# Weight sums for pairs of column tiles: made by GpSimd from loaded tiles, or made in DRAM by adding transfers and loaded as blocks

## The chip, the core and the metric

The kernel runs on one NeuronCore of a Trainium2 chip. The metric is the device time of one execution in microseconds, taken as the median of several runs. Beside it stands one profiled execution, from which all views below come.

## The reference

One layer of a hybrid decoder, 512 tokens of 1024 channels, all in float32. What matters here is which weights meet which activations:

```python
u = rmsnorm(h, norm1_g)
a_glu, q, k, v, r, g_low, gate_a, gate_b = split_cols(u @ w_in)
c = silu(layernorm(causal_dwconv(a_glu[..., :CH] * sigmoid(a_glu[..., CH:]), ...)))
y_conv = c @ w_conv_out
o = gated_linear_attention(q, k, v, log_sigmoid(g_low @ w_gate_up + b_gate) / 16)
y_gla = (headnorm(o) * silu(r)) @ w_gla_out
merged = sigmoid(gate_a) * y_conv + sigmoid(gate_b) * y_gla
h = h + merged @ w_o
u2 = rmsnorm(h, norm2_g)
z = causal_dwconv(u2 @ w_ffn_up, ...)                # 2 x 2816 columns
h = h + (silu(z[..., :F]) * z[..., F:]) @ w_ffn_down
return rmsnorm(h, final_g)
```

## The kernel before, in words

**Products.** Each float32 product is made of three matmuls: both operands are split into a high part (`hi`, a cast by ScalarE) and a low part (`lo`, a subtraction by VectorE), and `mm3` (L453 to L455) multiplies low by high, high by low and high by high into one bank. A weight comes in blocks of 128 partitions x 1024 values (512 KB): a column tile holds the 8 k-blocks of 128 output columns.

**The stream of weight blocks.** `order` lists all 202 blocks in the order of their use, by name: value, GLU, decay, the four attention heads (`w_qk`, `w_r`), the merge gates and the two branch projections (`w_gb`, `w_ga`, `w_gla`, `w_conv`), `w_o`, and three groups of `w_up` and `w_down`. `load` issues the next block's DMA on SyncE's queue into one of four `raw` buffers; `split_weight` makes its two parts into one of four `whi` and four `wlo` buffers; `weight` hands a block to TensorE's loops, splits two blocks ahead (`LOOK`), and lets `refill` load up to four blocks beyond the split ones. So a load waits for the buffer of the block four loads before it, that is, for that block's cast and subtraction.

**The pairs.** Twelve gate tiles and sixteen up-projection tiles, 14 pairs in all (six in `MERGE`, eight `w_up` pairs), are multiplied two at a time with the tokens in two halves by a scheme of seven block products in place of eight (`two_tiles`, L1174). For the tiles p and q, cut into left and right halves of their columns in the block, it needs four steps: x1 (tile p itself), x3 (two sums), x2 (a sum, and the right half of q) and x4 (one sum). In the kernel before, `load` takes both tiles of the pair into two `raw` buffers at step x1, and `two_sums` (L329) lets GpSimd make the four sums, each 128 x 512, into a third buffer and into q's left half, after the blocks are split; `two_operand` names the buffer of each step. While pairs are in the stream (`tight`), only two blocks are loaded ahead in place of four.

**Other users of the queues.** GpSimd also issues adding transfers (`accum_op=ALU.add`): the low parts of some blocks (`ADDED`, L393: the transfer adds the weight onto the negated high part), and the sums of blocks of `w_o` and `w_down` (L305, L322). It takes the inverse roots of the norms (L505, L608, L1592). SyncE issues all plain loads and the stores of the output.

**The start.** Under a hand-written order (`manual_schedule`), the first tile of x is loaded in two halves, then the first weight block in two halves (`load(2)`), the second tile of x, and two more blocks. TensorE first transposes x (L581) and multiplies as parts arrive (L667).

Of the kernel before, what the change touches and what calls it, by code (L numbers as in the profile page):

```python
# [10 lines left out]
F32 = mybir.dt.float32  # L11
# [4 lines left out]
ALU = mybir.AluOpType  # L16

P = 128
D = 1024
T = 512  # L20
# [18 lines left out]
BEHIND = [_HALVES[:3], _HALVES[3:6], _HALVES[6:9], _HALVES[9:]]  # L39
BEHIND += [[("w_conv", m, half) for m in pair for half in range(2)] for pair in O_PAIRS[:2]]  # L40
MERGE_REST = [("w_conv", m) for pair in O_PAIRS[2:] for m in pair]
LOOK = 2

ADDED = {("w_glu", 2 * k) for k in range(2, KT)} | {("w_r", m) for m in range(KT)}
# [31 lines left out]
def trunk_layer(ctx: ExitStack, tc: tile.TileContext, a: dict, out: bass.AP):  # L76
    nc = tc.nc

    def pool(name, bufs, space=None):
        kw = {"space": space} if space is not None else {}  # L80
        return ctx.enter_context(tc.tile_pool(name=name, bufs=bufs, **kw))
# [9 lines left out]
    up = pool("acts", 1)  # L91
    tp = pool("temps", 1)
    ps = pool("psum", 1, bass.MemoryType.PSUM)
    edge = ctx.enter_context(tc.tile_pool(name="edge", bufs=1, side="right"))
    heap_scope, hp = scoped("heap", 26)
    conv_scope, vp = scoped("conv", 10)
# [4 lines left out]
    def nm(s):  # L101
        return f"{s}_{next(names)}"
# [115 lines left out]
    tight = set()  # L218
    first = len(order)
# [4 lines left out]
    tight |= set(range(first, len(order)))  # L224
    order += MERGE_REST
    order += [("w_o", (O_PAIRS, step, d)) for step, d in STEPS]
    for gi, pairs in enumerate(GROUPS):
        if gi == 0:
            order += [("w_up", j) for i in pairs[0] for j in (i, FT + i)]
            first = len(order) + 6  # L230
        else:
            first = len(order)
        order += up_order(up_plan(gi))
        tight |= set(range(first, len(order)))
        order += [("w_down", (pairs, step, d)) for step, d in STEPS]
    ready, raws = [], []
    pair_raws = {}
    kept = {}
    used = [0]
    pace = [None]  # L240

    def by_halves(dst, src, parts):
        for j in range(parts):
            c = slice(j * D // parts, (j + 1) * D // parts)
            nc.sync.dma_start(dst[:, c], src[:, c])

    def load(parts=1):
        if len(raws) < len(order):
            name, j = order[len(raws)]
            if name in SEVEN:  # L250
                raws.append(load_block(name, *j))
                return
            if name == "two":
                name, p, q, part = j
                if part == "x1":
                    pair_raws[name, p] = [raw_tile() for _ in range(2)]
                    for raw, m in zip(pair_raws[name, p], (p, q)):
                        nc.sync.dma_start(raw, a[name][m])
                raws.append(None)
                return  # L260
            raw = raw_tile()
            by_halves(raw, a[name][j], parts)
            raws.append(raw)

    def refill():

        while len(raws) < len(order):
            if len(raws) >= len(ready) + (2 if len(raws) in tight else 4):
                return
            load()  # L270

    def raw_tile():
        return wp.tile([P, D], F32, tag="raw", name=nm("raw"), bufs=4)
# [36 lines left out]
    def operand(raw, pairs, step, d):  # L310

        if step == "s4":
            return kept[pairs, d, "b22"]
        if step == "n2":
            nc.vector.tensor_tensor(kept[pairs, d], kept[pairs, d], raw, ALU.add)  # L315
        return raw if step in ("a12", "n3") else kept[pairs, d]

    def sum_on(name, pairs, step, d):

        if step in ("a11", "n2"):  # L320
            nxt = block(name, pairs, d, *((0, 1) if step == "a11" else (1, 0)))
            nc.gpsimd.dma_start(kept[pairs, d], nxt, accum_op=ALU.add)  # L322

    def two_operand(name, p, q, part):

        raws = pair_raws[name, p]
        return {"x1": lambda: raws[0], "x3": lambda: raws[2], "x2": lambda: raws[1], "x4": lambda: raws[2][:, :T]}[part]()

    def two_sums(name, p, q, part):  # L329

        def add(out, x, y):
            work = nc.gpsimd.tensor_tensor(out, x, y, ALU.add)  # L332
            if name == "w_up":
                tc.keep_in_program_order(work)

        left, right = slice(0, T), slice(T, D)
        if part == "x1":
            one, two = pair_raws[name, p]
            three = raw_tile()
            pair_raws[name, p].append(three)  # L340
            add(three[:, left], one[:, left], two[:, left])
            add(three[:, right], three[:, left], two[:, right])
            add(two[:, left], two[:, left], two[:, right])
        if part == "x3":
            one, _, three = pair_raws[name, p]
            add(three[:, left], three[:, right], one[:, right])

    def split_weight(halves=False, between=None):

        if len(ready) < len(order):  # L350
            while len(raws) <= len(ready):
                load()
            raw = raws[len(ready)]
            name, spec = order[len(ready)]
            if name in SEVEN or name == "two":
                raw = operand(raw, *spec) if name in SEVEN else two_operand(*spec)
# [3 lines left out]
                nc.scalar.copy(hi, raw)  # L360
                two_low[:] = [nc.vector.tensor_tensor(lo, raw, hi.bitcast(F32), ALU.subtract)]  # L361
                with ExitStack() as order_of:
                    for ins in behind:
                        order_of.enter_context(tc.issue_after(ins.ins))
                    sum_on(name, *spec) if name in SEVEN else two_sums(*spec)
# [12 lines left out]
            lo = wp.tile([P, D], F32R, tag="wlo", name=nm("wlo"), bufs=4)  # L378
            if halves:
                ready.append((hi, lo))  # L380

                def high(c):
                    nc.scalar.copy(hi[:, c], raw[:, c])

                def low(c):
                    nc.vector.tensor_tensor(lo[:, c], raw[:, c], hi[:, c].bitcast(F32), ALU.subtract)

                cols = [slice(j * T, (j + 1) * T) for j in range(2)]
                return [[lambda c=c, part=part: part(c) for c in cols] for part in (high, low)]
            nc.scalar.copy(hi, raw)  # L390
            if (name, spec) in ADDED:
                pace[0] = nc.scalar.mul(lo, raw, -1.0)  # L392
                nc.gpsimd.dma_start(lo, a[name][spec], accum_op=ALU.add)  # L393
            else:
                pace[0] = nc.vector.tensor_tensor(lo, raw, hi.bitcast(F32), ALU.subtract)  # L395
# [153 lines left out]

    def load_x(t, parts=1):  # L550
        xs[t] = tp.tile([P, D], F32, tag="x", name=nm("x"), bufs=3)
        by_halves(xs[t], a["x"][t * P : (t + 1) * P, :], parts)

    def by_four(t):
        return t.rearrange("p (k t) -> p k t", k=4)
# [1223 lines left out]
```

## Time and profile before

| what | value |
|---|---|
| median of 3 runs | 826.51 us (826.05 to 828.54) |
| the profiled execution | 825.89 us |
| its span, first to last instruction | 824.2 us |
| granted TensorE clock | 0.999 |
| DMA packets | 30905, 106.27 MB |

The views give times in us from the start of the span. PE is TensorE, PEld its weight loads, DVE VectorE, ACT ScalarE, POOL GpSimd, SP SyncE; a q behind an engine's name is its sequencer, which waits and issues DMAs. A row of a view names line, engine, operation, the tile written and those read; an arrow in brackets names what ended the wait before it.

### The profile page before, as it was taken

Reading aid. Unit: us, or ns where it says so; the run is one execution under the profiler, and the core shown is the slowest. Engines: PE = TensorE matmul, PEld = TensorE weight load, DVE = VectorE, ACT = ScalarE, POOL = GpSimd, SP = SyncE. Lnnn points to the kernel's source line nnn. Section 1 sums busy time; section 2 is a strip of 40 time slices with the busy share of each in tenths; the row PEclk is TensorE's granted clock in tenths of the full one; section 3 lists DMA queues with packets and bytes.
Section 4 is the critical chain, followed back from the end, with each engine's and each line's share of the span. In section 5 each row is a group of like instructions: output and inputs, shape, how many; then the busy total and the mean of one; then the engine's idle time right before and its main releaser. Section 6 shows DMA issues by size and latency. Waiting matters only on the chain.

```text
span 824.2 us, 11554 instructions
## 1 busy us (share of the span) xinstructions
PE 815.3 (99%) x4321; PEld 705.2 (86%) x4321; DVE 715.7 (87%) x1161; ACT 450.2 (55%) x666; POOL 150.1 (18%) x133
## 2 busy tenths in 40 slices
PE   8999999999999999999999999999999999999996
PEld 7888888888888889999988898898889988899885
DVE  6689999999989599786788889979975999789896
ACT  6744447655654456684454546556435663456654
POOL 2000010001010213533001100230133301522012
PEclk9999999999999999999999999999999999999999
DMA  8345572563443103323647623156642457334662
GB/s 315 104 118 147 148 187 101 129 153 103 93 112 103 51 27 111 119 78 106 206 116 216 196 80 103 31 169 157 139 133 90 141 140 164 106 103 165 168 129 103
DMA packets 30905, 106.27 MB, mean 129 GB/s; under 512 B 3497, under 2 KB 3633, under 8 KB 30849
## 3 DMA queue, kind: packets, MB, share of 16 engines
q1 hardware_dynamic: 25072, 85.34, 30.4%
q0 software_dynamic: 5760, 20.19, 14.5%
q8 instruction: 34, 0.56, 0.3%
q14 instruction: 23, 0.18, 0.1%
q10 hardware_dynamic: 16, 0.00, 0.0%
HBM read 103.42 MB, written 2.10 MB: 128 GB/s over the span
## 4 chain that ended last, share of the span: by engine, by line
PE 98%; DMA 1%; ACT 0%; SPq 0%; DVE 0%; POOL 0%; issue 0%; POOLq 0%; ACTq 0%
PE mm L453 28%; PE mm L454 28%; PE mm L455 28%; PE mm L667 3%; PE ax L455 2%; PE ax L453 2%; PE ax L454 2%; PE ax L1070 1%; DMA x<-in_x_dram 1%; PE ax L1072 1%; PE ax L1051 1%; PE ax L1038 0%; PE ax L1037 0%; PE ax L534 0%; PE ax L581 0%; PE ax L1085 0%
## 5 line engine op out<-in xcount | busy, mean ns | idle before, releaser
L453 PE MATMUL mm<-uh,wlo 128*128 128x512 f32 (+1 forms) x672 | 244.5, 364 | 0.0
L454 PE MATMUL mm<-ul,whi 128*128 128x512 f32 (+1 forms) x672 | 242.3, 361 | 0.0
L455 PE MATMUL mm<-uh,whi 128*128 128x512 f32 (+1 forms) x672 | 242.1, 360 | 0.0
L455 PEld LDWEIGHTS mm<-uh,whi 128*128 128x128 f32 x672 | 126.8, 189 | 19.5
L453 PEld LDWEIGHTS mm<-uh,wlo 128*128 128x128 f32 x672 | 127.0, 189 | 18.8
L454 PEld LDWEIGHTS mm<-ul,whi 128*128 128x128 f32 x672 | 127.0, 189 | 18.6
L390 ACT CAST whi<-raw 128x1024 fp32r<-128x1024 f32 x86 | 89.9, 1048 | 59.2 <-PE mm L455 33.2
L361 DVE TENSOR_TENSOR wlo<-raw,whi 128x1024 fp32r<-128x1024 f32 x80 | 94.0, 1181 | 25.2 <-ACT whi L360 21.3
L332 POOL TENSOR_TENSOR raw<-raw,raw 128x512 f32<-128x512 f32 x42 | 67.9, 1616 | 213.9 <-DVE wlo L361 118.2
L395 DVE TENSOR_TENSOR wlo<-raw,whi 128x1024 fp32r<-128x1024 f32 x70 | 90.0, 1288 | 15.3 <-ACT whi L390 15.3
L360 ACT CAST whi<-raw 128x1024 fp32r<-128x1024 f32 x80 | 76.4, 958 | 35.7 <-PE mm L455 26.8
L791 DVE SCALAR_TENSOR_TENSOR c<-h,pp,c 128x255 f32<-128x255 f32 (+14 forms) x120 | 57.4, 478 | 3.7 <-ACT c L787 3.4
L791 DVE SCALAR_TENSOR_TENSOR c<-aside,btmp,c 128x255 f32<-128x255 f32 (+14 forms) x120 | 57.4, 478 | 2.8 <-ACT c L787 2.7
L791 DVE SCALAR_TENSOR_TENSOR aside<-h,pp,aside 128x255 f32<-128x255 f32 (+6 forms) x112 | 53.6, 478 | 0.0
L360 ACT CAST whi<-kept 128x1024 fp32r<-128x1024 f32 (+1 forms) x32 | 31.8, 997 | 31.3 <-DVE kept L315 17.3
L1503 DVE SCALAR_TENSOR_TENSOR tmp<-mm,pp,tmp 128x511 f32<-128x511 f32 (+1 forms) x56 | 41.4, 743 | 4.0 <-ACT tmp L1500 3.9
L361 DVE TENSOR_TENSOR wlo<-kept,whi 128x1024 fp32r<-128x1024 f32 (+1 forms) x32 | 36.9, 1154 | 5.1 <-ACT whi L360 5.1
L1181 ACT COPY tmp<-mm 128x256 f32<-128x256 f32 x48 | 17.7, 368 | 35.1 <-PE mm L455 34.6
L1419 DVE TENSOR_TENSOR hres<-hres,mm 128x512 f32<-128x512 f32 (+1 forms) x49 | 32.3, 671 | 3.8 <-PE mm L455 2.2
L1500 ACT ACTIVATE tmp<-mm,pp 128x512 f32<-128x512 f32 x28 | 21.8, 778 | 19.0 <-PE mm L455 18.8
L392 ACT ACTIVATE wlo<-raw 128x1024 fp32r<-128x1024 f32 x16 | 16.9, 1060 | 22.1 <-PE mm L453 22.1
L1503 DVE SCALAR_TENSOR_TENSOR tmp<-tmp,pp,tmp 128x511 f32<-128x511 f32 (+1 forms) x32 | 27.8, 888 | 0.4
(350 smaller groups left out, 1787.5 us busy)
## 6 DMA issues: line engine op xcount, KB each, us to landing
raw<-in_w_up_dram SPq DMA_DIRECT2D x44, 512.0 KB, 3.7
raw<-in_w_glu_dram SPq DMA_DIRECT2D x16, 512.0 KB, 4.8
raw<-in_w_down_dram SPq DMA_DIRECT2D x15, 512.0 KB, 4.8
kept<-in_w_down_dram POOLq DMA_DIRECT2D x10, 512.0 KB, 5.8
raw<-in_w_qk_dram SPq DMA_DIRECT2D x8, 512.0 KB, 3.4
raw<-in_w_r_dram SPq DMA_DIRECT2D x8, 512.0 KB, 4.4
wlo<-in_w_r_dram POOLq DMA_DIRECT2D x8, 512.0 KB, 7.8
raw<-in_w_gb_dram SPq DMA_DIRECT2D x8, 512.0 KB, 3.3
```

Of the source, the lines that this page charges most:

```text
L332: work = nc.gpsimd.tensor_tensor(out, x, y, ALU.add)
L360: nc.scalar.copy(hi, raw)
L361: two_low[:] = [nc.vector.tensor_tensor(lo, raw, hi.bitcast(F32), ALU.subtract)]
L390: nc.scalar.copy(hi, raw)
L395: pace[0] = nc.vector.tensor_tensor(lo, raw, hi.bitcast(F32), ALU.subtract)
L453: nc.tensor.matmul(acc, ll, rh, start=first, stop=False, **kw)
L454: nc.tensor.matmul(acc, lh, rl, start=False, stop=False, **kw)
L455: nc.tensor.matmul(acc, lh, rh, start=False, stop=last, **kw)
L667: nc.tensor.matmul(acc, act, ready[k // 2][wi][:, j], start=first, stop=last)
L791: nc.vector.scalar_tensor_tensor(out[:, j:], x[:, : half_t - j], w, out[:, j:], ALU.mult, ALU.add)
L1419: done = nc.vector.tensor_tensor(hres[t, n][:, c], hres[t, n][:, c], acc[:, c], op)
L1503: nc.vector.scalar_tensor_tensor(z[:, s:], acc[:, : T - s], w[j], z[:, s:], ALU.mult, ALU.add)
```

## The change

For each pair, a tile `s` of four blocks of 128 x 512 is set up in DRAM. `sum_two` gives four stages: two copies from DRAM to DRAM of the tiles p and q, issued on SyncE's queue; one adding transfer of 512 KB (the halves of q onto blocks 0 and 2); and two of 256 KB that add blocks of `s` onto one another, issued by GpSimd, each after the one before it has landed. `SUMS_AT` gives the block at whose use the stages begin, for each pair; the next three stages follow three blocks apart. `load_two` then loads each step's block into a `raw` buffer of its own: x1 from p, x3 from `s` in one transfer, x2 half from `s` and half from q in two transfers, x4 (256 KB) from `s`. GpSimd's sums on SBUF, `tight` and the bound of two blocks go: up to four blocks are loaded ahead everywhere. The first weight block is loaded in one transfer; the first tile of x still in two.

```diff
+SUMS_AT = (26, 30, 34, 38, 42, 46, 52, 60, 68, 76, 101, 109, 137, 145)
...
+    dp = pool("dram", 1, bass.MemoryType.DRAM)
...
-                if part == "x1":
-                    pair_raws[name, p] = [raw_tile() for _ in range(2)]
-                    for raw, m in zip(pair_raws[name, p], (p, q)):
-                        nc.sync.dma_start(raw, a[name][m])
-                raws.append(None)
+                raws.append(load_two(*j))
                 return
             raw = raw_tile()
-            by_halves(raw, a[name][j], parts)
+            nc.sync.dma_start(raw, a[name][j])
             raws.append(raw)
     def refill():
-        while len(raws) < len(order):
-            if len(raws) >= len(ready) + (2 if len(raws) in tight else 4):
-                return
+        while len(raws) < min(len(ready) + 4, len(order)):
             load()
...
-    def two_sums(name, p, q, part):
-        def add(out, x, y):
-            work = nc.gpsimd.tensor_tensor(out, x, y, ALU.add)
-            if name == "w_up":
-                tc.keep_in_program_order(work)
-        left, right = slice(0, T), slice(T, D)
-        if part == "x1":
-            one, two = pair_raws[name, p]
-            three = raw_tile()
-            pair_raws[name, p].append(three)
-            add(three[:, left], one[:, left], two[:, left])
-            add(three[:, right], three[:, left], two[:, right])
-            add(two[:, left], two[:, left], two[:, right])
-        if part == "x3":
-            one, _, three = pair_raws[name, p]
-            add(three[:, left], three[:, right], one[:, right])
+    def sum_two(name, p, q):
+        s = dp.tile([P, 4, T], F32, name=nm("sums"))
+        two_in_dram[name, p] = s
+        def copies():
+            for j, m in ((0, p), (2, q)):
+                tc.keep_in_program_order(nc.sync.dma_start(s[:, j : j + 2, :], by_two(a[name][m])))
+        def add(dst, src):
+            tc.keep_in_program_order(nc.gpsimd.dma_start(dst, src, accum_op=ALU.add))
+        return [
+            copies,
+            lambda: add(s[:, 0:4:2, :], by_two(a[name][q])),
+            lambda: add(s[:, 3, :], s[:, 0, :]),
+            lambda: add(s[:, 1, :], s[:, 3, :]),
+        ]
+    def by_two(x):
+        return x.rearrange("p (j c) -> p j c", j=2)
+    def load_two(name, p, q, part):
+        raw = raw_tile()
+        if part == "x1":
+            nc.sync.dma_start(raw, a[name][p])
+            return raw
+        s = two_in_dram[name, p]
+        if part == "x3":
+            nc.sync.dma_start(by_two(raw), s[:, 0:4:3, :])
+        if part == "x2":
+            nc.sync.dma_start(raw[:, :T], s[:, 2, :])
+            nc.sync.dma_start(raw[:, T:], a[name][q][:, T:])
+        if part == "x4":
+            raw = raw[:, :T]
+            nc.sync.dma_start(raw, s[:, 1, :])
+        return raw
+    for first, (name, p, q) in zip(SUMS_AT, twos):
+        for stage in range(4):
+            two_stages.setdefault(first + 3 * stage, []).append((name, p, q, stage))
+    def sums_in_dram():
+        for name, p, q, stage in two_stages.pop(used[0], ()):
+            if stage == 0:
+                two_jobs[name, p] = sum_two(name, p, q)
+            two_jobs[name, p][stage]()
...
         used[0] += 1
+        sums_in_dram()
         prefetch(ahead)
...
     load_x(0, 2)
-    load(2)
+    load()
     load_x(1)
```

The order in which TensorE and VectorE run their instructions is the same in both kernels; ScalarE's differs by one swap. SyncE's and GpSimd's orders differ as described.

More of the change, by code (lines that the diff above doesn't have):

```diff
@@ L217, in trunk_layer @@
     order += [("w_gb", m) for m in range(AHEAD)] + [("w_gla", m) for m in range(AHEAD - 1)]
-    tight = set()
-    first = len(order)
     for (name, p, q), behind in zip(MERGE, BEHIND):
@@ L223, in trunk_layer @@
             order += [tile[:2] for tile in behind[n : n + 1] if tile[2] == 0]
-    tight |= set(range(first, len(order)))
     order += MERGE_REST
@@ L229, in trunk_layer @@
             order += [("w_up", j) for i in pairs[0] for j in (i, FT + i)]
-            first = len(order) + 6
-        else:
-            first = len(order)
         order += up_order(up_plan(gi))
-        tight |= set(range(first, len(order)))
         order += [("w_down", (pairs, step, d)) for step, d in STEPS]
     ready, raws = [], []
-    pair_raws = {}
     kept = {}
@@ L240, in trunk_layer, with load @@
     pace = [None]
[L242 to L247, printed above, removed]
+    def load():
         if len(raws) < len(order):
@@ L322, in sum_on @@
             nc.gpsimd.dma_start(kept[pairs, d], nxt, accum_op=ALU.add)
-    def two_operand(name, p, q, part):
-        raws = pair_raws[name, p]
-        return {"x1": lambda: raws[0], "x3": lambda: raws[2], "x2": lambda: raws[1], "x4": lambda: raws[2][:, :T]}[part]()
-    def two_sums(name, p, q, part):
-        def add(out, x, y):
-            work = nc.gpsimd.tensor_tensor(out, x, y, ALU.add)
-            if name == "w_up":
-                tc.keep_in_program_order(work)
-        left, right = slice(0, T), slice(T, D)
-        if part == "x1":
-            one, two = pair_raws[name, p]
-            three = raw_tile()
-            pair_raws[name, p].append(three)
-            add(three[:, left], one[:, left], two[:, left])
-            add(three[:, right], three[:, left], two[:, right])
-            add(two[:, left], two[:, left], two[:, right])
-        if part == "x3":
-            one, _, three = pair_raws[name, p]
-            add(three[:, left], three[:, right], one[:, right])
+    two_in_dram = {}
@@ new lines, in trunk_layer @@
+    two_stages = {}
+    twos = [j[:3] for what, j in order if what == "two" and j[-1] == "x1"]
+    assert len(twos) == len(SUMS_AT)
+    for first, (name, p, q) in zip(SUMS_AT, twos):
+        for stage in range(4):
+            two_stages.setdefault(first + 3 * stage, []).append((name, p, q, stage))
+    two_jobs = {}
+    def sums_in_dram():
[3 more added lines that the diff above has]
+            two_jobs[name, p][stage]()
@@ L355, in split_weight @@
             if name in SEVEN or name == "two":
-                raw = operand(raw, *spec) if name in SEVEN else two_operand(*spec)
+                raw = operand(raw, *spec) if name in SEVEN else raw
                 n = raw.shape[-1]
@@ L361, in split_weight @@
                 two_low[:] = [nc.vector.tensor_tensor(lo, raw, hi.bitcast(F32), ALU.subtract)]
[L362 to L365, printed above, removed]
+                if name in SEVEN:
+                    sum_on(name, *spec)
                 ready.append((hi, lo))
@@ L551, in load_x @@
         xs[t] = tp.tile([P, D], F32, tag="x", name=nm("x"), bufs=3)
-        by_halves(xs[t], a["x"][t * P : (t + 1) * P, :], parts)
+        for j in range(parts):
+            c = slice(j * D // parts, (j + 1) * D // parts)
+            nc.sync.dma_start(xs[t][:, c], a["x"][t * P : (t + 1) * P, c])
     def by_four(t):
```

1 line of the change is left out of this document (removed).

## The prediction

> **What bounds the kernel now.** I read the page first: busy time per engine, then the chain that ended last.
>
> ```profile
> span 824.2 us, 11554 instructions
> ## 1 busy us (share of the span) xinstructions
> PE 815.3 (99%) x4321; PEld 705.2 (86%) x4321; DVE 715.7 (87%) x1161; ACT 450.2 (55%) x666; POOL 150.1 (18%) x133
> ...
> PE 98%; DMA 1%; ACT 0%; SPq 0%; DVE 0%; POOL 0%; issue 0%; POOLq 0%; ACTq 0%
> ```
>
> TensorE works 815.3 of 824.2 us, and 98% of the chain is its own. A busy TensorE can still wait between matmuls, so I asked the view of waits for that engine alone, over the whole span, and the same for its weight loads after the first 28 us:
>
> ```profile
> PE mm L573 <- DVE ones L546: 1.1, 1, 1.1
> PE mm L667 <- ACT whi L383: 0.7, 1, 0.7
> PE ax L581 <- DMA x<-in_x_dram: 0.2, 1, 0.2
> ```
>
> ```profile
> PEld mm L454 <- DVE wlo L361: 0.2, 1, 0.2
> ```
>
> These are all the waits there are: 0.7 and 0.2 us in the first 9 us, behind the first weight block and the second tile of x (the 1.1 us is the launch), and 0.2 us once, late. TensorE never waits for a sum that GpSimd made. So nothing between the start and the end can be won; the question is what the change makes it wait for. The stages in which the pairs of the merge and the output projection run, in the table of windows (us, then busy us of PE, PEld, DVE, ACT, POOL, granted clock, DMA share, GB/s):
>
> ```profile
> 286.00:345.00 59.00, 59.00 (x361) 53.01 (x360) 54.51 (x72) 34.39 (x53) 19.02 (x11) 1.00 0.26 81
> 345.00:400.00 55.00, 55.00 (x366) 50.69 (x365) 42.33 (x54) 37.04 (x56) 18.91 (x12) 1.00 0.31 103
> 400.00:435.00 35.00, 35.00 (x182) 30.02 (x181) 26.31 (x40) 15.09 (x23) 1.76 (x2) 1.00 0.59 157
> 435.00:480.00 45.00, 45.00 (x223) 38.05 (x222) 38.96 (x54) 24.48 (x38) 6.52 (x8) 1.00 0.68 197
> ```
>
> TensorE fills each one at full clock, and the DMA engines have room: a quarter to two thirds busy.
>
> **The change, part by part.** *Removed: GpSimd's sums.* The costliest groups of POOL:
>
> ```profile
> L332 POOL TENSOR_TENSOR raw<-raw,raw 128x512 f32<-128x512 f32 x42 | 67.9, 1616 | 213.9 <-DVE wlo L361 118.2 <-DVE wlo L395 42.2 <-DVE hres L1419 22.1
> L332 POOL TENSOR_TENSOR raw<-raw 128x512 f32<-128x512 f32 x14 | 27.2, 1945 | 0.0
> L322 POOL DMA_DIRECT2D kept<-in_w_down_dram x12 | 10.4, 867 | 60.0 <-DVE wlo L361 52.9 <-ACT tmp L1500 5.2 <-ACT whi L360 2.0
> ```
>
> Four adds for each of 14 pairs go, 67.9 + 27.2 = 95.1 us of GpSimd; 14 x 3 adding transfers come, at 0.867 us of issue each 36.4 us. GpSimd is 18% busy, so neither is time. VectorE may run some subtractions faster without those adds beside it, but no matmul waits for one (0.2 us once): worth 0 to 0.2 us, taken as 0.
>
> [...]
>
> *Added: transfers.* The DMA queues, and the issues with KB each and median us to landing:
>
> ```profile
> q1 hardware_dynamic: 25072, 85.34, 30.4%
> q0 software_dynamic: 5760, 20.19, 14.5%
> ...
> kept<-in_w_down_dram POOLq DMA_DIRECT2D x10, 512.0 KB, 5.8
> ...
> wlo<-in_w_r_dram POOLq DMA_DIRECT2D x8, 512.0 KB, 7.8
> raw<-in_w_gb_dram SPq DMA_DIRECT2D x8, 512.0 KB, 3.3
> ...
> out_dram<-y SPq DMA_DIRECT2D x2, 512.0 KB, 2.6
> ```
>
> SyncE's queue q1 costs 0.304 x 824.2 / 85.34 = 2.94 us of all engines for a MB, GpSimd's q0, which is adding transfers, 0.145 x 824.2 / 20.19 = 5.92. A pair now copies 2 x 0.524 = 1.05 MB in DRAM, adds 0.524 + 0.262 + 0.262 = 1.05 MB, and loads 3 x 0.524 + 0.262 = 1.83 MB instead of 1.05. That is 1.05 x 2.94 + 1.05 x 5.92 + 0.79 x 2.94 = 11.6 us of DMA for a pair, 162 us for 14: the mean share rises from 0.45 to 0.65. No row shows a transfer from DRAM to DRAM; if its writing costs as much again as its reading, copies and adds double, and the share is 0.81. In 286 to 435 us the present work is 0.26 x 59 + 0.31 x 55 + 0.59 x 35 = 53 us of 149; six pairs' larger loads (6 x 2.3 = 14 us) and about 4.5 pairs' sums (4.5 x 9.3 = 42, doubled 84) make it 109 to 151. So on average there is room, with none to spare at the upper bound.
>
> *Lead.* An average does not decide; the latest block does. The sums themselves can't be late: in the order of the changed program the last add of a pair is issued ten weight blocks or more before its load. What can be late is a load queued behind a pair's two copies, which SyncE issues in its one order. The case with the least lead that I found is the x2 block of the merge pair (4, 5) of w_ga: four buffers back in the ring is a tile whose low part is done at 366.24 + 0.69, which frees the buffer; the cast of the x2 block stands at 372.94; the first matmul with it at 383.72:
>
> ```profile
> 366.24 0.69 DVE L361 TENSOR_TENSOR wlo<-raw,whi 128x512 fp32r<-128x512 f32 x1 [1.70 <-ACT whi L360]
> ```
>
> ```profile
> 372.94 1.06 ACT L360 CAST whi<-raw 128x1024 fp32r<-128x1024 f32 x1
> ```
>
> ```profile
> 383.72 0.28 PE L453 MATMUL mm<-sumsq,wlo 128*128 128x256 f32 x1
> ```
>
> The lead to the cast is 6.0 us, to the matmul 16.8; cast and subtraction need 1.06 + 1.2, so 14.5 us may pass before TensorE stands. In the changed order two copies stand just ahead of this load. A copy reads and writes: 3.3 us (a load alone) to 5.9 (load 3.3, then the store's 2.6). Two that overlap like loads, 2 x 0.524 x 2.94 = 3.1 us, and then the load's 3.3 to 5.6, are 6.4 to 8.7; two one after the other, 11.8 plus 5.6, are 17.4. The 5.6 is a load beside adding transfers, in 450 to 470 us:
>
> ```profile
> raw<-in_w_up_dram SPq DMA_DIRECT2D x4, 512.0 KB, 5.6
> ```
>
> I take 8.7, since every row of q1 shows transfers that overlap. The cast then is up to 3 us late and TensorE, with 5.8 us left, is not. This cover is gone if copies go one by one: 17.4 + 1.4 of issue (three at 0.45) against 14.5 is a stall of 4.3 us. I add 0.3 us for it (an estimate).
>
> [...]
>
> *Moved: the first weight block in one transfer.* ScalarE's rows, TensorE's and SyncE's at the start:
>
> ```profile
> 5.82 0.62 ACT L383 CAST whi<-raw 128x512 fp32r<-128x512 f32 x1 [3.11 <-DMA raw<-in_w_v_dram]
> 6.34 0.61 ACT L594 CAST h<-h 128x512 fp32r<-128x512 f32 x1
> 7.55 0.62 ACT L383 CAST whi<-raw 128x512 fp32r<-128x512 f32 x1 [0.59 <-DMA raw<-in_w_v_dram]
> 8.08 1.05 ACT L601 ACTIVATE junk<-x 128x1024 bf16<-128x1024 f32 x1
> 9.04 0.19 ACT L601 ACTIVATION_READ_ACCUMULATOR junk<-x 128x1 f32 x1
> 10.12 1.14 ACT L383 CAST whi<-raw 128x512 fp32r<-128x512 f32 x2 [0.89 <-DMA raw<-in_w_v_dram]
> ```
>
> ```profile
> 8.22 0.50 PE L667 MATMUL mm<-whi,h 128*128 128x512 f32 x1 [0.72 <-ACT whi L383]
> 8.90 1.10 PE L581 MATMUL ax<-ident,x 128*128 128x128 f32 x8 [0.18 <-DMA x<-in_x_dram]
> ```
>
> ```profile
> 1.72 0.90 SPq L245 DMA_DIRECT2D raw<-in_w_v_dram x2
> ```
>
> Now no cast can start on the first half at 5.82; both wait for the whole block, between 7.55 less one issue (0.90 / 2 = 0.45), 7.1, and 7.55. From 7.4: cast, cast of h, cast at spacings of 0.52, so the second is done at 7.4 + 1.04 + 0.62 = 9.06 instead of 8.17, and the transposes of 8.90 move to some 9.3. ScalarE's 1.05 + 0.19 then end at 10.25 and push the cast of 10.12 by 0.15; from there everything follows in one line. Against this, one issue less lets later blocks land up to 0.45 sooner. So the start is worth -0.45 to +0.9 us; I take +0.2, nearest to ScalarE's row at 10.12.
>
> *Sum.* The profiled execution took 825.89 us (span 824.2 and 1.7 around it), 0.6 under the median of the three runs, 826.51, so changes are put on the median: 826.51 + 0 + 0.3 + 0.2 = 827.0.
>
> **The rivals.** *Late blocks (slower).* Copies and adds hold a load longer than its lead. It decides once two copies and a load take over 14.5 us after the buffer is free. For it: the shares of 0.59 and 0.68 above, which the adds raise; no row shows a copy. Against it: the 5.8 us left at the overlapping rate. Seven of the 14 pairs' copies stand among loads of pairs; if two hit as hard as this one, 2 x 4.3 = 8.6 us: 826.5 + 0.2 + 8.6 = 835.3; one hit 831.
>
> *GpSimd's order (slower).* An add waits for the one before it to land, and in the attention stage GpSimd's low-part adds of w_r and its roots are queued behind. If an add in DRAM takes 7.8 + 3.3 = 11.1 us rather than 5.8 to 7.8, three take 33 us, which is more than a head's four blocks; some 1.5 us for each of the four heads would give 832.7. Against it: the copies are issued blocks ahead, and each add has three blocks.
>
> *Faster.* The start's waits of 0.7 + 0.2 vanish with the earlier landing, and nothing else can: 825.6. That is still no measurable gain.
>
> **How the numbers follow.** A measurement here can tell 0.3%, 2.5 us (824.0 to 829.0), from no change. Forecast, no stall worth it: 0.63, between 825.8 (the start's -0.45 and some) and 828.9 (start +0.9, a third of a hit twice). Late blocks 0.23, GpSimd's order 0.11, both past 829; over 0.3% faster 0.03, for something unseen. The likeliest time is 827.0; the range goes from 825.8 to 834.0, which leaves out the upper half of the slower cases and a few in a hundred below: under 2 in 10.
>
> **What would show it.** Right: TensorE's waits after 28 us stay under 1 us in all, its busy time within 2 us of 815.3; the DMA share near 0.65 or above; the first cast near 7.4. Wrong: waits of TensorE for casts, low parts or ScalarE's copies out of the banks between 310 and 420 or 620 and 700 us, with loads of raw that take over 10 us to land (late blocks); or casts that wait for wlo of w_r, and POOL waiting for DMA sums in 140 to 285 us (GpSimd's order). A gain of over 2.5 us would mean that TensorE's rate itself depends on something beside it, which no row here shows.

## The result, and the profile after

| | before | changed |
|---|---|---|
| median, lowest to highest of 22 runs each | 826.39 us (825.31 to 829.85) | 829.49 us (826.12 to 833.77) |
| profiled execution, its span | 825.89 us, 824.2 us | 829.51 us, 827.7 us |
| granted TensorE clock of that execution | 0.999 | 0.994 |

The ratio is 1.0028, with a 95% interval of 1.0018 to 1.0039: 2.3 us slower (1.5 to 3.2), on the edge of what counts as no change (0.3%). The ratio is worked out over all runs and is not the quotient of the medians, which lie 3.1 us apart. One later run of the kernel before took 1231 us at a granted clock of 0.627; it stands alone and is left out of all ratios. The forecast was 827.0 us, so the loss is real, larger than the 0.5 us foreseen, and it has to be found. The changed kernel's times spread more than those of the kernel before; the price comes in some executions and not in others.

The page of the changed kernel, with the busy times, the granted clock in 40 slices and the two queues:

```profile
span 827.7 us, 11690 instructions
...
PE 817.1 (99%) x4321; PEld 706.5 (85%) x4321; DVE 692.0 (84%) x1161; ACT 449.5 (54%) x666; POOL 93.1 (11%) x119
...
PEclk8999999999999999999999999999999999999999
...
q1 hardware_dynamic: 36800, 111.04, 39.7%
q0 software_dynamic: 13600, 34.87, 26.5%
```

GpSimd is relieved as the change intends (150.1 to 93.1 us), VectorE a little (715.7 to 692.0), and the DMA engines carry 0.397 + 0.265 = 0.66 of their time in place of 0.45. TensorE is 1.8 us longer busy, and its clock is short of full in the first slice. Its waits, over the whole span, and its weight loads' after 28 us:

```profile
PE mm L685 <- ACT h L612: 2.8, 1, 2.8
PE mm L591 <- DVE ones L562: 1.1, 1, 1.1
PE mm L469 <- ACT whi L405: 0.5, 1, 0.5
```

```profile
PEld mm L469 <- ACT whi L405: 0.9, 1, 0.9
PEld mm L470 <- DVE wlo L378: 0.2, 1, 0.2
```

There are two new places: 2.8 us at the start, and 0.5 us near 705 us. The windows say that there is no third. The columns are those of the prediction (busy us of PE first, granted clock, DMA share and GB/s last). First the kernel before, then the changed one:

```profile
8.00:16.00 8.00, 7.60 (x38) 6.30 (x39) 6.37 (x10) 6.46 (x12) 0.15 (x1) 1.00 0.95 375
28.00:690.00 662.00, 662.00 (x3505) 572.39 (x3505) 583.45 (x975) 360.18 (x530) 112.47 (x87) 1.00 0.44 123
690.00:760.00 70.00, 70.00 (x418) 62.46 (x417) 60.77 (x78) 36.32 (x53) 22.86 (x14) 1.00 0.44 134
```

```profile
8.00:16.00 8.00, 7.25 (x25) 6.11 (x26) 6.94 (x11) 6.69 (x12) 0.00 (x0) 0.57 0.97 381
28.00:690.00 662.00, 662.00 (x3510) 572.67 (x3509) 565.87 (x976) 358.19 (x529) 75.81 (x83) 1.00 0.69 180
690.00:760.00 70.00, 69.51 (x406) 61.30 (x405) 54.94 (x78) 37.02 (x53) 2.62 (x3) 1.00 0.52 157
```

From 28 to 690 us TensorE is busy for all 662 us in both, with 0.69 of the DMA engines in use in place of 0.44: the stretch in which all copies, all adds of sums and almost all blocks of the pairs run costs TensorE nothing while it lasts. At 8 to 16 us the granted clock is 0.57. ScalarE's and TensorE's rows of the start, changed kernel:

```profile
7.56 0.62 ACT L398 CAST whi<-raw 128x512 fp32r<-128x512 f32 x1 [4.85 <-DMA raw<-in_w_v_dram]
8.60 0.61 ACT L398 CAST whi<-raw 128x512 fp32r<-128x512 f32 x1
```

```profile
5.12 0.83 PE L591 MATMUL mm<-ones 128*128 128x128 f32 x6
8.75 1.32 PE L685 MATMUL mm<-whi,h 128*128 128x512 f32 x2 [2.80 <-ACT h L612]
9.86 1.48 PE L599 MATMUL ax<-ident,x 128*128 128x128 f32 x6
28.19 1.03 PE L599 MATMUL ax<-ident,x 128*128 128x128 f32 x8
```

The warm-up matmuls (L591) end at 5.95 us, and TensorE has nothing until 8.75. The transposes of the second tile of x begin at 9.86, 0.96 us later than the 8.90 of before. But those of the third tile, which stood at 24.91 in the kernel before, are 3.28 us late. The 2.3 us between are the clock: it was full from 4.68 us on, fell to half (0.50) at 8.10 for 6.83 us, two steps of 3.41, and was full again from 14.92. In the kernel before it was full from 6.63 to 822.41 us, past the last matmul at 817.21.

So the theory was: the whole first block makes TensorE wait, and the wait costs more in clock than in waiting. The rival: the sums' traffic costs the time, and the start 1 us at most.

### The profile page after: what moved, and what is told of

Read it like the earlier page. It is cut to its first block, busy times and chain, and to the rows that moved or that the text cites. A ratio compares the mean times of both kernels' runs of the same rounds, so it can differ in the third digit from the quotient of the medians.

```text
span 827.7 us, 11690 instructions
## 1 busy us (share of the span) xinstructions
PE 817.1 (99%) x4321; PEld 706.5 (85%) x4321; DVE 692.0 (84%) x1161; ACT 449.5 (54%) x666; POOL 93.1 (11%) x119
## 4 chain that ended last, share of the span: by engine, by line
PE 98%; DMA 1%; ACT 0%; DVE 0%; issue 0%; POOL 0%; SPq 0%; POOLq 0%; ACTq 0%
PE mm L469 28%; PE mm L470 28%; PE mm L471 28%; PE mm L685 3%; PE ax L471 2%; PE ax L470 2%; PE ax L469 2%; PE ax L1088 1%; DMA raw<-in_w_v_dram 1%; PE ax L1090 1%; PE ax L1069 1%; PE ax L1056 0%; PE ax L599 0%; PE ax L1055 0%; PE ax L550 0%; PE ax L1103 0%
## 5 line engine op out<-in xcount | busy, mean ns | idle before, releaser
L378 DVE TENSOR_TENSOR wlo<-raw,whi 128x1024 fp32r<-128x1024 f32 x80 | 88.1, 1107 | 36.5 <-ACT whi L377 32.5
L410 DVE TENSOR_TENSOR wlo<-raw,whi 128x1024 fp32r<-128x1024 f32 x70 | 85.2, 1220 | 15.8 <-ACT whi L405 15.8
L321 POOL DMA_DIRECT2D sums<-sums x28 | 24.9, 919 | 111.4 <-DMA sums<-in_w_up_dram 65.4
L470 PE MATMUL mm<-wlo,sh 128*128 128x512 f32 x66 | 25.8, 390 | 0.0
```

The source lines that it names most:

```text
L321: tc.keep_in_program_order(nc.gpsimd.dma_start(dst, src, accum_op=ALU.add))
L470: nc.tensor.matmul(acc, lh, rl, start=False, stop=False, **kw)
```

## The experiments

Each kernel was timed beside the kernel before on the same chip; the e, f and g kernels ran on three different chips. "Difference" is between the medians; the ratio, over all runs, has its 95% interval, and where a few runs are long the two can differ in sign (g1).

| kernel | median us | before | difference | ratio |
|---|---|---|---|---|
| e1_halves | 826.92 | 826.72 | +0.2 | 1.0004 (0.9989 to 1.0019) |
| e2_whole_alone | 828.49 | 826.72 | +1.8 | 1.0014 (0.9998 to 1.0029) |
| e3_warm | 826.10 | 826.72 | -0.6 | 0.9994 (0.9984 to 1.0005) |
| e4_warm_before | 826.29 | 826.72 | -0.4 | 0.9988 (0.9978 to 0.9999) |
| f1_changed_again | 828.75 | 827.13 | +1.6 | 1.0025 (1.0007 to 1.0042) |
| f2_before_warm | 826.43 | 827.13 | -0.7 | 0.9992 (0.9983 to 1.0001) |
| f3_sums_halves_warm | 827.44 | 827.13 | +0.3 | 1.0013 (0.9996 to 1.0029) |
| f4_copies_doubled | 831.91 | 827.13 | +4.8 | 1.0047 (1.0028 to 1.0067) |
| g1_fewer_loads_ahead | 827.00 | 827.28 | -0.3 | 1.0008 (0.9993 to 1.0022) |
| g2_less_warm_before | 828.07 | 827.28 | +0.8 | 1.0009 (0.9998 to 1.0020) |
| g3_doubled_fewer_loads | 828.80 | 827.28 | +1.5 | 1.0026 (1.0012 to 1.0041) |
| g4_changed_fewer_loads | 827.80 | 827.28 | +0.5 | 1.0020 (1.0002 to 1.0038) |

Differences of under 1 us between two rows are within the intervals, and e2's interval too just reaches no change; what follows rests on the larger differences and, above all, on the profiles.

### One part at a time: e1_halves and e2_whole_alone

The first puts the halves back into the changed kernel, the second puts the whole block into the kernel before:

```diff
# e1, in the changed kernel
-            nc.sync.dma_start(raw, a[name][j])
+            for n in range(parts):
+                c = slice(n * D // parts, (n + 1) * D // parts)
+                nc.sync.dma_start(raw[:, c], a[name][j][:, c])
...
     load_x(0, 2)
-    load()
+    load(2)
# e2, in the kernel before
     load_x(0, 2)
-    load(2)
+    load()
```

> The changed kernel with the first weight block in two transfers again; the sums stay in DRAM. Theory (the start costs the 3 us: TensorE waits 2.8 us for the whole block and its clock then falls to half for one or two windows of 3.41 us): the first matmul is at about 7.0 us again, the granted clock stays full from there, and the time is 826.4 to 827.2 us, what is left over the kernel before being the single late load near 701 us (0.65 us). Rival (the traffic of the sums costs the 3 us, and the start 1 us at most): 828.5 to 829.5 us.

> The kernel before with the first weight block in one transfer, and nothing else changed: GpSimd makes the sums. Theory: TensorE's first wait for a cast grows to 2 to 3 us, the granted clock is at half for some windows of 3.41 us between 8 and 16 us, and the time is 828.0 to 830.0 us, with runs spread over 4 us by where the windows fall. Rival (the sums' traffic is the cause): 826.3 to 827.4 us.

Both came out by the theory: the sums alone +0.2 us, the whole block alone +1.8. The whole block without any sum in DRAM shows the wait, the clock and the late transposes, here in the views of waits, windows and TensorE's rows of e2:

```profile
PE mm L667 <- ACT h L594: 1.7, 1, 1.7
```

```profile
8.00:16.00 8.00, 7.25 (x30) 5.92 (x31) 7.48 (x12) 7.31 (x14) 0.10 (x1) 0.79 0.96 381
```

```profile
9.59 1.04 PE L581 MATMUL ax<-ident,x 128*128 128x128 f32 x8
27.09 1.04 PE L581 MATMUL ax<-ident,x 128*128 128x128 f32 x8
```

The transposes are 0.69 us late at 9.59, and 2.18 at 27.09: one step of 3.41 us at half clock cost 1.5 us. One thing was not as expected: in e1's profiled execution the first half block itself came late (its cast at 6.68 in place of 5.82), TensorE waited 1.8 us, and the clock was at half from 8.20 for one step (0.79 in the mean of 8 to 16 us). So the kernel before probably has this cost too, in those executions in which its data come late; its granted clocks, below, point to it.

### The clock or the wait: e3_warm, e4_warm_before, f2_before_warm, g2_less_warm_before

If the clock is the cost, TensorE only has to be given something to do while it waits. `WARM` counts calls of the warm-up loop; each call shows as two matmuls in the profile, so 3 and 11 calls, which the expectations name as 3 and 11 matmuls, are its 6 and 22 matmuls:

```diff
# e3, in the changed kernel; f2, the same in the kernel before
-WARM = (5, 3, 2)
+WARM = (5, 11, 2)
# e4, in the kernel before
-WARM = (5, 3, 2)
+WARM = (5, 4, 2)
...
-    by_parts(accs[0], 0, (0, 1), (HH,))
+    by_parts(accs[0], 0, (0,), (HH,))
+    warm(2)
+    by_parts(accs[0], 0, (1,), (HH,))
+    warm(1)
# g2, in the kernel before
-WARM = (5, 3, 2)
+WARM = (5, 0, 2)
```

> The changed kernel with 11 in place of 3 warm-up matmuls in the second of the three bursts at the start, so that TensorE has work while it waits for the first cast; the whole first block and the sums in DRAM stay. Theory: no half clock between 8 and 16 us, so only the later start itself is left, about 1 us: 827.2 to 828.2 us, and little spread. Rival 1 (the sums' traffic): no change, 829 to 830 us. Rival 2 (the 2.8 us of waiting themselves, not the clock): 829 to 830 us at a full clock.

> The kernel before with a few more warm-up matmuls around its first matmuls (one more in the second burst, a burst of two and one of one behind the first two early matmuls), to fill its own short waits of 0.7 and 0.2 us. If what spread there is in its times (825.3 to 829.9) comes from a clock that falls in these waits: 825.8 to 826.3 us and less spread. Rival (its waits are too short to touch the clock): 826.3 to 827.0 us, the same or slightly slower by the added matmuls.

> The kernel before with 11 in place of 3 warm-up matmuls in the second burst: halves, GpSimd's sums, no wait at the start. Theory (half clock in the waits of the start also makes the spread of the kernel before, 824.9 to 831.1): median 825.7 to 826.3 us, highest under 828.5 us, clock 0.997 or more in nearly all executions. Rival (the spread comes from elsewhere, the data's landing for instance): median 826.3 to 827.3 us and single executions past 829 us.

> The kernel before with no warm-up matmuls in the second burst; data, transfers and casts unchanged, so no matmul of the work is later for want of data. TensorE is idle from about 5.5 to 7.0 us and again for 0.7 us. Theory (idle time near one window of the clock halves it): half clock for one or two windows of 3.41 us in most executions, 828.0 to 830.0 us. Rival (the wait for data costs, not the clock): 826.5 to 827.2 us, as the kernel before.

With 22 warm-up matmuls in place of 6 the changed kernel takes 826.10 us, less than even the theory expected: in these 11 runs the loss is gone, with the whole block and the sums in DRAM still there. (f3 and g1 below, with the same warm-up and the sums, do have runs past 830 us, for another reason.) Its waits over the whole span, and TensorE at 8 to 16 us:

```profile
PE mm L591 <- DVE ones L562: 1.1, 1, 1.1
```

```profile
8.00:16.00 8.00, 8.00 (x45) 6.81 (x44) 6.54 (x12) 6.82 (x12) 0.55 (x1) 1.00 0.95 367
```

In this execution the first block also came early (first cast at 6.24), so the profile by itself doesn't separate waiting from clock. The 11 runs do, with 827.84 us as their highest, and so does g3 below: there the block came at 7.64, as late as in the changed kernel, and with the same 22 warm-up matmuls the wait was 0.4 us and the clock stayed full (1.00 from 8 to 16 us).

The kernel before gains from it as well. With the warm-up, f2's 12 runs lie between 825.51 and 827.63 us (standard deviation 0.6) and e4's 11 between 825.23 and 827.33 (0.6), against 825.31 to 829.30 (1.1) of the kernel before beside f2 and 824.90 to 831.14 (1.4) beside e4. The granted clock goes with it: over 104 runs of the kernel before, those with a granted clock of 0.998 or 0.999 took 826.4 us in the mean (50 runs), with 0.997 827.4 (34), with 0.995 or 0.996 828.5 (20). e4's interval lies just under 1: it is the best version that the experiments gave, by 0.1%, which is hardly a gain.

g2 goes the other way: no transfer moves, only the six warm-up matmuls go. The clock then was not full until 14.14 us: the first two matmuls of the work took 0.80 and 0.79 us (0.49 and 0.50 before), and the eight transposes took almost twice as long as the 1.10 us of before:

```profile
9.20 1.94 PE L581 MATMUL ax<-ident,x 128*128 128x128 f32 x8
```

Its median is 0.8 us above the kernel before, at the low edge of what the theory expected; the interval reaches to no loss. (In g2's profiled execution the first half came late too, with a wait of 1.9 us.)

### The price of the sums: f1_changed_again, f3_sums_halves_warm

f1 is the changed kernel as it is. f3 has all three: sums in DRAM, halves as in e1, warm-up as in e3, so that against f2 only the sums differ.

> The changed kernel once more, beside the next three on one chip, so that all four have the same neighbour. Both theories: 828.5 to 829.8 us, with most executions between clock 0.994 and 0.998.

> The changed kernel's sums in DRAM, with the first block in halves and 11 warm-up matmuls. Against the kernel before with the same warm-up this is the price of the sums in DRAM alone. Theory (the sums cost nothing that shows): within 0.5 us of it. Rival (the sums' traffic costs): 1.0 to 3.0 us above it.

f1 repeats the result beside new runs of the kernel before (+1.6 us, 1.0025). f3 is 1.0 us above f2 by the medians, between the two theories, and has single executions up to 833.51 us, where f2 ends at 827.63: the rival is not dead. The profile fell on that worst one and shows the place at once. Waits of TensorE, f3, then the same of f1:

```profile
PE mm L471 <- DVE hres L1439: 5.0, 1, 5.0
```

```profile
PE mm L469 <- DVE hres L1437: 2.6, 1, 2.6
```

Again it is one wait, at 701 to 707 us, where the changed kernel had 0.5. ScalarE stands there, by its rows in f3, for tiles into which GpSimd's adding transfers put two blocks of `w_down`; the casts of the next `w_up` block stand behind it in ScalarE's order:

```profile
702.94 1.04 ACT L379 CAST whi<-kept 128x1024 fp32r<-128x1024 f32 x1 [5.39 <-DMA kept<-in_w_down_dram]
704.94 0.62 ACT L379 CAST whi<-kept 128x512 fp32r<-128x512 f32 x1 [0.95 <-DMA kept<-in_w_down_dram]
```

In f3 these two transfers were issued late, and they landed late. GpSimd's rows from 672 to 695 us, the kernel before, then f3. For the same place in the work, add 0.80 us to the times of the kernel before: SyncE issues its next `w_up` load at 692.67 there and at 693.47 in f3.

```profile
681.04 0.86 POOL L305 DMA_DIRECT2D raw<-in_w_down_dram  x1 [7.73 <-DVE al L1523]
688.31 0.87 POOL L305 DMA_DIRECT2D raw<-in_w_down_dram  x1 [6.41 <-DVE hres L1419]
689.52 0.85 POOL L322 DMA_DIRECT2D kept<-in_w_down_dram  x1 [0.34 <-DVE wlo L361]
690.72 0.89 POOL L322 DMA_DIRECT2D kept<-in_w_down_dram  x1 [0.35 <-DVE wlo L361]
```

```profile
672.53 1.24 POOL L323 DMA_DIRECT2D sums<-sums  x1
...
685.16 0.84 POOL L290 DMA_DIRECT2D raw<-in_w_down_dram  x1 [10.48 <-DVE hres L1439]
692.57 0.88 POOL L290 DMA_DIRECT2D raw<-in_w_down_dram  x1 [6.57 <-DVE hres L1439]
693.12 2.09 POOL L307 DMA_DIRECT2D kept<-in_w_down_dram  x2
```

The delay begins 20 us earlier. At 672.53 an add of a sum is issued; at 674.65 SyncE issues a plain load of `w_down` into a `raw` buffer. Its landing, the kernel before and f3:

```profile
raw<-in_w_down_dram SPq DMA_DIRECT2D x1, 512.0 KB, 6.5
```

```profile
raw<-in_w_down_dram SPq DMA_DIRECT2D x1, 512.0 KB, 9.8
```

The adding transfer into this buffer is issued 0.7 us after the plain load has landed, in both; so it stands at 685.16 in f3, 3.3 us late. The next plain load then runs beside it and lands in 6.1 us in place of 2.7, the next add into `raw` is 3.5 us late, and the adds into `kept` behind it in GpSimd's order are 2.8 and 2.2 us late. They land in 9.7 and 11.2 us in place of 6.3 and 8.0. What is also new is one load: SyncE issues four in this stretch (the x3 block from `sums` takes the place of the pair's second tile, and a `w_up` tile follows it) where the kernel before issues three. After f3's wait of 5 us the clock went to half for 3.41 us too, at 707.34 (0.98 in the mean of 690 to 760 us).

### Is there lead left, and do the early loads matter: f4, g1, g3, g4

```diff
# f4, in the changed kernel with the warm-up of e3
     s = dp.tile([P, 4, T], F32, name=nm("sums"))
+    again = dp.tile([P, 4, T], F32, name=nm("again"))
...
     tc.keep_in_program_order(nc.sync.dma_start(s[:, j : j + 2, :], by_two(a[name][m])))
+    tc.keep_in_program_order(nc.sync.dma_start(again[:, j : j + 2, :], by_two(a[name][m])))
# g1 (on f3), g3 (on f4), g4 (on the changed kernel)
-        while len(raws) < min(len(ready) + 4, len(order)):
+        third = order.index(("two", ("w_up", 14, 36, "x3")))
+        while len(raws) < min(len(ready) + (2 if len(raws) in (third, third + 1) else 4), len(order)):
```

> The changed kernel with 11 warm-up matmuls (826.1 us), and each pair's two copies made twice, the second time into a tile that nobody reads: four copies stand on SyncE's queue ahead of the next load in place of two, 14.7 MB more traffic each way. By the lead worked out before (14.5 us from the buffer to the matmul): two copies and a load measured about 6 and 5.5 us; if four overlap at the same rate they take 9 us, with the load 14.5, just the lead, so 826.0 to 827.5 us with waits of TensorE under 1 us after 28 us. Rival (no lead is left, the late blocks are near): waits of 1 to 4 us at several of the 14 pairs, 829 to 840 us.

> Sums in DRAM, first block in halves, 11 warm-up matmuls (827.4 us median, single executions past 830), and now at one place the old bound: the x3 block of the third group's first pair and the tile behind it are loaded only when all but two of the blocks before them are split, so they no longer stand beside the adding transfers into kept near 693 us. Theory (what is left of the sums' price is these two early loads, which hold the adding transfers into kept up to 11 us): no wait at 701 us, adding transfers of 6 to 8 us there, 826.0 to 826.7 us with all executions under 829. Rival (the sums' traffic costs by itself, or DRAM is slow there whatever is loaded): still 827 to 828 us, with single executions past 830.

> The kernel with every copy made twice (831.9 us median) and the same bound on the two loads near 693 us. Theory (the doubled copies stretch the lead elsewhere only by the waits of 0.3 to 0.7 us seen at 410 and 660 us): 826.7 to 828.3 us. Rival (the copies themselves are late for the blocks): 830 us or more.

> The changed kernel as it is (whole first block, 3 warm-up matmuls) with the bound on the two loads alone. Theory (two causes that add, the start and the place near 701 us): what is left is the start, 827.8 to 828.8 us, with no wait at 701 us. Rival (the start is all): no change, 828.7 to 829.5 us.

The line that puts the bound back had no effect. Every engine of g1 runs the same instructions in the same order as in f3, and so do g3 and f4, g4 and the changed kernel. SyncE's loads near 701 us in the changed kernel, then in g4, stand the same distances apart (2.93 and 3.53 us after the first):

```profile
695.95 0.33 SPq L247 DMA_DIRECT2D raw<-in_w_up_dram  x1
...
698.88 0.38 SPq L341 DMA_DIRECT2D raw<-sums  x1
699.48 0.33 SPq L247 DMA_DIRECT2D raw<-in_w_up_dram  x1
```

```profile
694.95 0.33 SPq L247 DMA_DIRECT2D raw<-in_w_up_dram  x1
...
697.88 0.38 SPq L342 DMA_DIRECT2D raw<-sums  x1
698.48 0.33 SPq L247 DMA_DIRECT2D raw<-in_w_up_dram  x1
```

So g1, g3 and g4 don't test the early loads; they are repeats of f3, f4 and the changed kernel on another chip, and their gains (1.0013 to 1.0008, 1.0047 to 1.0026, 1.0025 to 1.0020) say only how far such repeats differ. That their profiles have no wait near 701 us is no answer to the expectations. g1 and g4 still have single executions of 831.11 and 833.49 us.

f4 is 4.8 us slower, in the range of the rival, but mostly not by its mechanism: the longest wait of its profile is once more the one place (3.5 us, and the clock at half from 707.53, 0.98 in the mean of 690 to 760 us). g3, the same instructions again, took 828.80 us; by these two medians the kernel with doubled copies costs 1.5 to 4.8 us over the kernel before. Its profile has no wait near 701 us, and what is left is one wait near 660 us, where the cast of a block from `sums` waits 3.4 us for its load. The waits of g3, then ScalarE's row:

```profile
PE mm L472 <- ACT tmp L1202: 1.2, 1, 1.2
PE mm L594 <- DVE ones L565: 1.1, 1, 1.1
PE mm L688 <- ACT h L615: 0.4, 1, 0.4
```

```profile
658.34 1.05 ACT L380 CAST whi<-raw 128x1024 fp32r<-128x1024 f32 x1 [3.42 <-DMA raw<-sums]
```

So the lead is real but not large: two more copies ahead of a load use it up there.

What the repeats are good for is the wait near 701 us, since fourteen profiles now show the place. All times in us from the issue of the first `w_up` load there (692.67 in the kernel before); they are differences of issue and landing times in the traces:

| kernel | first add into `raw` issued | adds into `kept` issued | second one landed | wait |
|---|---|---|---|---|
| before; e2; e4; f2; g2 (sums by GpSimd) | -12.7 to -11.6 | -3.15, -1.95 | 4.7 to 6.6 | none; e2 0.2 |
| g1 | -10.6 | -3.20, -1.95 | 5.0 | none |
| g3 | -10.4 | -3.03, -1.95 | 5.0 | none |
| changed | -10.3 | -3.20, -1.95 | 6.9 | 0.5 |
| g4 | -10.0 | -2.86, -1.95 | 6.1 | none |
| e3 | -9.9 | -2.88, -1.95 | 5.3 | none |
| e1 | -9.5 | -2.44, -1.90 | 7.2 | 0.9 |
| f4 | -9.3 | -2.01, -1.47 | 9.9 | 3.5 |
| f1 | -9.2 | -2.20, -1.66 | 9.0 | 2.6 |
| f3 | -8.3 | -0.34, 0.20 | 11.4 | 5.0 |

Two things can be read from it. Wherever there is a wait, it is the landing of the second add into `kept` less 6.4 us, in all six profiles that have one; the profiled execution of the kernel before, at 6.0, had 0.4 us to spare. And all kernels with sums in DRAM issue the first add into `raw` later than any without; the four that issue it last are the four with a wait of 0.9 us or more, and the only ones in which the second add into `kept` is issued later than -1.95. The extra load can't be the whole cause: it is there in g1, g3 and e3 too, and their adds into `kept` landed in 6.4 to 7.3 us, no later than in the kernels before (6.1 to 8.6). So the place and the chain of waits are shown. That the add of a sum at 672 us starts the chain is likely, and not settled: no run moved it. Why the plain load beside it lands in 7.5 us in g1 and in 9.8 in f3 is open.

## Why the prediction was right or wrong

*What bounds the kernel* held: nothing in the middle could be won, and 23.7 us less of VectorE and 57.0 less of GpSimd moved no matmul. GpSimd's new issues are 0.91 us each in place of 0.867, which does not matter.

*DMA cost* held: 0.66 of the DMA engines against the 0.65 forecast, so the writing in DRAM did not double the price.

*Lead* held, and at the block that was worked out. SyncE's rows of the changed kernel at the x2 block of the merge pair (4, 5), and ScalarE's cast of it; times are 3.28 us later than before:

```profile
366.81 1.14 SPq L318 DMA_DIRECT2D sums<-in_w_up_dram  x2
369.10 0.33 SPq L343 DMA_DIRECT2D raw<-sums  x1
369.47 0.57 SPq L344 DMA_DIRECT2D raw<-in_w_ga_dram  x1
```

```profile
raw<-sums SPq DMA_DIRECT2D x1, 256.0 KB, 5.9
raw<-in_w_ga_dram SPq DMA_DIRECT2D x1, 256.0 KB, 6.1
```

```profile
376.22 1.05 ACT L377 CAST whi<-raw 128x1024 fp32r<-128x1024 f32 x1
```

From the first load's issue at 369.10 the block is there at 369.47 + 6.1 = 375.6, so 6.5 us against the 8.7 taken (bounds 6.4 to 17.4). The copies had been issued 2.3 us ahead of the load, at 366.81; from there it is 8.8 us. The copies took 6.8 us each (the median of the two), so they overlapped with each other and with the loads. The cast stands at 372.94 + 3.28 = 376.22, where it would have been anyway.

*The allowance of 0.3 us for a stall* was near as a middle value, by luck and for the wrong place. The sums alone cost 0.2 us (e1) to 1.0 (f3 over f2) by the medians, but as a wait of 0 to 5.0 us at 701 us. What the prediction left out are the adding transfers into `kept`. It sought the least lead among loads behind copies, with 14.5 us to go; here the lead was 0.4 us. It priced the 42 new adding transfers by GpSimd's time and the share of the DMA engines, and did not ask which transfers they stand beside: loads held up by adds, and adds held up by late loads.

*The start* is the step that failed. Its first part came near: the first cast at 7.56 against 7.4, the second done at 9.21 against 9.06. The transposes were to be at 9.3 and came at 9.86, 0.3 of it since the two matmuls before them took 1.32 us at half clock (1.02 in e2, still at full). Then came 2.3 us more by the clock, so the term of +0.2 (bounds -0.45 to +0.9) was 3.3 us in the profiled execution and 1.8 by the medians of e2. The prediction costed a late TensorE at its lateness alone. The trace had the clock, full from 6.63 us past the last matmul, and no sentence of the prediction asked what a longer wait does to it.

The changes of the clock stand whole steps of 3.41 us apart (8.10 to 14.92 us in the changed kernel are two). A wait shorter than a step was enough: at the start, steps with 1.7 to 2.4 us of waiting were followed by half clock (2.15 of the 2.8 us in the changed kernel, whose wait runs on into the next step), and in the changed kernel's profile a second step at half followed although TensorE had been idle for only 0.65 us of the first. Where in the step the wait falls differs between executions: f1's wait of 2.6 us near 701 us fell into two steps, 1.6 and 1.0 us, and left the clock full (1.00 from 690 to 760 us). How much of the spread comes from this, and how much from the data's landing, is not shown.

*The rivals.* Late blocks: the right kind of event in the window named (620 to 700 us), but not by its mechanism: no load of a pair came late, adding transfers did. That its 4.3 us a hit is near the 5.0 at worst is chance. GpSimd's order: not in the attention stage, since TensorE has no wait between 28 and 700 us; near 690 us adds that wait for what is ahead of them in GpSimd's order are part of the chain. Faster: not by the start.

*What would show it.* The waits after 28 us were to stay under 1 us in all; TensorE's own were 0.5 us in this execution and 2.6 in f1's. TensorE's busy time is within 2 us of 815.3, as said. The time, 829.49, is 2.5 us above the forecast and inside the range, but past the 828.9 to which the likeliest case reached: it lies in the part of the range that was kept for late blocks, which did not come as told, so that the range holds is partly luck. By the ratio of 1.0028 it is still no change within 0.3%, with an interval that reaches past it.

## What to carry to other kernels

Price a wait of TensorE by what it does to the clock, too: here a wait of 1.7 to 2.8 us at the start cost 1.5 to 2.3 us more at half clock, and eight more calls of a warm-up loop took it back and halved the spread of the times. Before transfers are added, look for the place with the least lead in the whole kernel, not only among the blocks that the change touches. When a change moves the median by the size of its own spread, take one part at a time, and read several profiles of the same place before believing in a stall. And look in the trace whether an edit has moved what it was meant to move: a better time alone doesn't show it.

## What was not expected of the hardware

The changes of the clock stand whole steps of 3.41 us apart: 239 from 6.63 to 822.41 us in the kernel before, 1, 2 and 237 between 4.68, 8.10, 14.92 and 823.88 in the changed one, 205 from 7.61 to 707.34 in f3. A step in which TensorE stood still for half the time (1.7 us in e2, 1.85 in e1) was followed by half clock; steps with 1.02 us (the kernel before) and 1.63 (f1, near 701 us) were not. The idle time alone did not decide: 1.88 us in f3, from 700.51 to 703.92, left the clock full. Of the steps at half clock, one with 0.33 us of idle time was followed by full clock (f1), those with 0.50 (g2) and 0.65 (the changed kernel) by half clock again. (The idle times go by the ends of matmuls, which the traces model.) An early full clock made it worse: in the changed kernel it came at 4.68 us, so six warm-up matmuls took 0.83 us in place of 1.37 and left a wait of 2.8 us (in e2, with the first cast at 7.54 us, they took 1.49 and left 1.7). The landing of the first half block differs by more than 1 us between executions (first cast at 5.27 us in g1, 5.43 in e4, 5.82 before, 6.84 in f3), and with it the wait.
